# Mixer groups in their own place: a hybrid encoder step with another order of TensorE's small work

## The chip, the cores and the metric

The kernel runs on one core of one Trainium2 chip. The metric is the device time of one execution in microseconds; the median over runs is compared. Matrix products run on TensorE, elementwise work on VectorE (DVE), ScalarE (ACT) and GpSimd (POOL), and most transfers are issued by SyncE (SP).

## The reference

One layer of a streaming encoder is applied to a prompt of 1024 tokens without history and to 32 tokens of a running stream with states. D is 1024. The mixer splits one input projection into three groups of heads, each of which runs a causal recurrence in blocks; the feed-forward part is a gated one with a causal convolution.

```
proj = rms_norm(x) @ w_in                     # split in 15 parts
o_a = gated_linear_scan(q, k, v, log_a, s)    # GLA: 6 heads, dk 32, dv 64
o_b = gated_linear_scan(q, k, v, log_f, s)    # HGRN2: 5 heads, 64 x 64
o_c = mlstm_scan(q, k, v, log_f, ig, c, n, m) # mLSTM: 5 heads, 64 x 64, matrix memory c
cat = concatenate([head_rms_norm(o_a) * silu(gr), head_rms_norm(o_b) * silu(hg),
                   head_rms_norm(o_c) * sigmoid(mo)])
x = x + rms_norm(cat @ w_out)
up = causal_dwconv(rms_norm(x) @ w_up)        # 2 x 2816 wide, 3 taps
x = x + rms_norm((gelu(gate) * val) @ w_down)
...
# inside a scan, per block of L = 64 tokens:
o = scores @ v + (q * exp(b)) @ S             # within the block, and from the state
S = exp(b_last) * S + (k * exp(b_last - b))^T @ v
```

It returns both outputs and all final states.

## The kernel before

**Stages.** The tokens go through the input projection in three groups (`inproj`, g = 0, 1, 2: three, three and two units of 128 prompt tokens, and the 32 sample tokens with the last). Then comes the output projection unit by unit (`outproj`), then the feed-forward part. Every big product is done in three matmuls on split operands (`mm3`: high by high L101, low L102 and L103). The order of units in the output projection is 0, 1, 2, 3, 8, 4, 5 and then 6, 7; unit 8 is the sample.

**Input projection.** Feature-major results are the tiles `pf`; token-major ones are `pv`. In the last group, `vg_across` computes a token-major block in two transposed halves (24 matmuls of 288 columns each, ScalarE copies a half to `vf`), and `back` transposes a whole block to tokens in `pb` (L455), from where `vg_store` passes it on: for the later blocks tanh on ScalarE, a VectorE step on the one tile `vth` (L429), a product on GpSimd (L431), and a store.

**Mixers.** The generator `mixer` runs the recurrence of one unit. `merge` pumps it as side work: units 0 to 2 beside the projection of group 1, units 3 to 5 beside group 2, units 8, 6, 7 beside the output projection. On TensorE a unit is a sequence of small groups: `sc_0`, `sc_2`, `sc_4` (scores at two levels of distance each; `keys`, `memory_scores` and `states` follow them as `mi` and `sm`), then `og` and `oh` (outputs of the two scans, with the memory update `mi` behind them), then `oi` and `om` (memory outputs: from the state `C`, and by the weights `w` within the block). VectorE writes masked scores into `P` (L807), which `og` reads. `finish` turns `og` and `oh` into rows of `cat`: square (ACT L989), sum (DVE L990), root (POOL L220, L221), product (DVE L992), gate (POOL L994). `om` and `oi` of a unit use the two buffers (tag "o") that `og` and `oh` leave after L992. `cat` goes to `cat_d` in memory and comes back as `ct`; `outproj` transposes it (`ctp`, L1076) for its products `zp`. Unit 7's `cat` stays in place. The next unit's `qkb` is loaded into a single buffer, and `qe` (ACT L814) is made from it.

**Order.** A scheduler simulates the program and, on each engine, takes the ready instruction with the lowest priority number; the number is the place in the program. `tc.high_priority(offset=n)` lowers it by n, and `tc.issue_after(x)` keeps an instruction behind x. All mixer matmuls go through `soon` (L717 to 719), which chains those of a group one behind the other.

Of the kernel before, what the change touches and what calls it, by code (L numbers as in the profile page):

```python
# [91 lines left out]
def body(ctx: ExitStack, tc: tile.TileContext, a: dict):  # L92
    nc = tc.nc
    act, dve, pool, pe, sp = nc.scalar, nc.vector, nc.gpsimd, nc.tensor, nc.sync
# [5 lines left out]
    def mm3(ps, lh, rh, first, last, **kw):  # L100
        pe.matmul(ps, lh[0], rh[0], start=first, stop=False, **kw)  # L101
        pe.matmul(ps, lh[0], rh[1], start=False, stop=False, **kw)  # L102
        return pe.matmul(ps, lh[1], rh[0], start=False, stop=last, **kw)  # L103
# [175 lines left out]
    def units_of(g):  # L279
        t0, pl, sl = GROUPS[g]  # L280
        us = [(t0 // 128 + i, 128 * i, 128) for i in range(pl // 128)]
        if sl:
            us.append((8, pl, sl))
        return us
# [72 lines left out]
    def inproj(g, xh, xl, normed, scaled=None):  # L357
# [47 lines left out]
        def vg_weights(blk):  # L405
            parts = [(a["w_tok0"][:, ks[0]:ks[-1] + 1], ks, lt0_d[:, ks[0]:ks[-1] + 1]) for ks in VG0] if not blk else \
                [(a["w_tok"][blk - 1, hf], range(4 * hf, 4 * hf + 4), lt_d[blk - 1, hf]) for hf in range(2)]
            ws = []
            for i, (src, ks, low) in enumerate(parts):
                wh, wl, _ = weights(src, p1, f"wt{g}_{blk}_{i}", [128, len(ks), 256 if blk else 282],  # L410
                                    raw=wraw.pop((blk, i), None), eng=dve if VGD[g](blk, i) else pool, low=low, kept=g > 0)
                ws += [(wh[:, k], wl[:, k]) for k in range(len(ks))]
            return ws

        def vg_store(blk, u, off, n, ps):
            o = mx.tile([128, 256], F32, tag="vg", name=f"vg{u}_{blk}", bufs=3)
            t = t0 + off
            if blk < 4:
                vcopies.append(act.copy(o[:n], ps[:n, :256]))
                act.dma_start(v_d[t:t + n, 256 * blk:256 * blk + 256], o[:n])  # L420
                return
            c0 = 256 * (blk - 4)
            th = mx.tile([128, 256], F32, tag="vth", name=f"vth{u}_{blk}", bufs=1)
            ia = tanh(th[:n], ps[:n, :256], 0.5)
            ns = min(max(704 - c0, 0), 256)
            if ns:
                iv = dve.scalar_tensor_tensor(th[:n, :ns], th[:n, :ns], 1.0, ps[:n, :ns], op0=ALU.add, op1=ALU.mult)
            if ns < 256:
                iv = dve.tensor_scalar(th[:n, ns:], th[:n, ns:], 1.0, None, op0=ALU.add)  # L429
            vgi[:] = ia, iv  # L430
            pool.tensor_tensor(o[:n], th[:n], gh[:n, c0:c0 + 256], op=ALU.mult)  # L431
            pool.dma_start(g_d[t:t + n, c0:c0 + 256], o[:n])
# [13 lines left out]
        def vg_across(blks):  # L446

            def back(blk, fs):
                us = units_of(g)
                whole = psb.tile([128, 2, 256], F32, tag="big", name=f"pb{us[0][0]}_{blk}")  # L450
                rest = psb.tile([128, 256], F32, tag="big", name=f"pb8_{blk}")
                pss = [whole[:, 0], whole[:, 1], rest]
                for (u, off, n), ps in zip(us, pss):
                    for e in range(2):
                        pe.transpose(ps[:n, 128 * e:128 * e + 128], fs[e][:, off:off + n], ident)  # L455
                for (u, off, n), ps in zip(us, pss):
                    vg_store(blk, u, off, n, ps)

            before = None
            for blk in blks:  # L460
                ws = vg_weights(blk)
                fs = p1.tile([128, 2, T], F32, tag="x", name=f"vf{blk}", bufs=3)
                fs = [fs[:, 0], fs[:, 1]]
                for e in range(2):
                    ps = psb.tile([128, T], F32, tag="big", name=f"pv{g}_{blk}_{e}")
                    for k in range(8):
                        mm3(ps, [w[:, 128 * e:128 * e + 128] for w in ws[k]], (xh[:, k, :], xl[:, k, :]), k == 0, k == 7)
                    act.copy(fs[e], ps)
                    if before and e:
                        back(*before)  # L470
                    yield
                before = (blk, fs)
                yield
            back(*before)
# [215 lines left out]
        if sl:  # L690
            yield from vg_across(range(1, 8))
            return
# [17 lines left out]
    AHEAD = 100  # L710
    LNA = 100

    SOON = 400

    line = [None]

    def soon(fn, *args, **kw):  # L717
        with tc.high_priority(offset=SOON), tc.issue_after(line[0].ins) if line[0] else ExitStack():
            line[0] = fn(*args, **kw)  # L719

    def mixer(u, g, ci0):
        n = 128 if u < 8 else DEC
        t0 = 128 * u
        chunks = [(0, 64), (64, 64)] if u < 8 else [(0, DEC)]
        cl = chunks[0][1]
# [16 lines left out]
        vmt = vm[0]  # L742
# [103 lines left out]
        def scores(sc, c, L, Q, at):  # L846
            for j in (3, 0, 1, 2):
                for (o, m) in chunks:
                    for hf in range(2):
                        f, q0, q1, p0 = HALVES[hf][j]  # L850
                        r = slice(64 * hf, 64 * hf + 64)
                        mm = c if c == levels[0] else m
                        soon(pe.matmul, sc[o:o + mm, p0:p0 + q1 - q0, at:at + m // 2], L[r, f, o:o + mm],
                             Q[r, q0:q1, o // 2:(o + m) // 2], start=True, stop=True)
# [6 lines left out]
        def keys():  # L861
            for f0 in (0, 2):
                kps = small(2, 128)
                for f in (f0, f0 + 1):
                    soon(pe.transpose, kps[:n, f - f0, :], khf[:, f * n:f * n + n], ident)
                for ch, (o, m) in enumerate(chunks):
                    with tc.high_priority(offset=AHEAD):
                        act.copy(kt2[o:o + m, ch, 128 * f0:128 * f0 + 256], kps[o:o + m].rearrange("p f n -> p (f n)"))

        w = mx.tile([128, 320], F32, tag="w", name=f"w{u}", bufs=1)  # L870
        w3 = w[:n, :5 * cl].rearrange("p (h n) -> p h n", n=cl)

        def memory_scores():
            sm = psm.tile([128, 6, 64], F32, tag="o", name=f"sm{u}", bufs=2)
            for f in range(3):
                rows, hs = (128, slice(2 * f, 2 * f + 2)) if f < 2 else (64, slice(4, 5))
                for (o, m) in chunks:
                    soon(pe.matmul, sm[o:o + m, hs, :m], mk[:rows, f, o:o + m], mqz[:rows, hs, o:o + m], start=True, stop=True)
            kp = small(4, 64)
            for f in range(2):  # L880
                soon(pe.transpose, kp[:n, 2 * f:2 * f + 2, :].rearrange("p h d -> p (h d)"), mk[:, f, :], ident)
            soon(pe.transpose, sm[:n, 5, :], mk[:64, 2, :], ident[:64, :64])
            for (h0, h1, kp) in ((0, 4, kp), (4, 5, sm[:, 5:6])):
                for ch, (o, m) in enumerate(chunks):
                    kwi[0] = dve.tensor_tensor(kw2[o:o + m, ch, h0:h1], kp[o:o + m, :h1 - h0],
                                               cols[o:o + m, 96 + h0:96 + h1].unsqueeze(2).broadcast_to([m, h1 - h0, 64]), op=ALU.mult)
            dve.tensor_tensor(w3, w3, sm[:n, :5, :cl], op=ALU.mult)
# [79 lines left out]
        for (h0, h1, ot) in ((0, 6, og), (6, 11, oh)):  # L967
            for h in range(h0, h1):
                f, r0, dk, vc = HEADS[h]
                for ch, (o, m) in enumerate(chunks):  # L970
                    soon(pe.matmul, ot[o:o + m, OUT[h], :], P[o:o + m, PLANE[h], :m], v[o:o + m, vc:vc + 64],
                         start=h == h0, stop=False, skip_group_check=True)
        for (h0, h1, ot) in ((0, 6, og), (6, 11, oh)):
            for h in range(h0, h1):
                f, r0, dk, vc = HEADS[h]
                for ch, (o, m) in enumerate(chunks):
                    soon(pe.matmul, ot[o:o + m, OUT[h], :], qz[:, h, o:o + m], Ss[ch][:, f, :],
                         start=False, stop=h == h1 - 1, skip_group_check=True)
# [23 lines left out]
        om = psm.tile([128, 5, 65], F32, tag="o", name=f"om{u}", bufs=2)  # L1002
        oi = psm.tile([128, 5, 65], F32, tag="o", name=f"oi{u}", bufs=2)
        line[0] = None
        for h in range(5):
            for ch, (o, m) in reversed(list(enumerate(chunks))):
                soon(pe.matmul, oi[o:o + m, h, :], mqz[:, h, o:o + m], Cs[ch][:, h // 2, :], start=True, stop=True)
        for h in range(5):
            for ch, (o, m) in enumerate(chunks):
                soon(pe.matmul, om[o:o + m, h, :], w[o:o + m, h * cl:h * cl + m], vmt[o:o + m, h, :], start=True, stop=True)  # L1010
        yield
        hn = mx.tile([128, 5, 65], F32, tag="hn", name=f"hn{u}", bufs=1)
        dve.tensor_tensor(hn[:n], oi[:n], cols[:n, 32:37].unsqueeze(2).broadcast_to([n, 5, 65]), op=ALU.mult)
# [677 lines left out]
    def mixers(g):  # L1691
        us = [(u, 2 * i) for i, (u, off, n) in enumerate(units_of(g))]
        return chain_of(*[mixer(u, g, c) for (u, c) in us[-1:] + us[:-1]]) if us[-1][0] == 8 else \
            chain_of(*[mixer(u, g, c) for (u, c) in us])
# [252 lines left out]
```

## Time and profile before

| | |
|---|---|
| median of 3 runs | 1396.19 us (1401.11, 1394.82, 1396.19) |
| profiled execution | 1395.19 us, span 1393.4 us |
| granted TensorE clock, mean | 0.979 |
| TensorE busy | 1316.8 us, 95% |
| VectorE / ScalarE / GpSimd busy | 1022.0 / 704.4 / 329.2 us |

Busy time of TensorE is matmuls; weight loads overlap them. A wait in brackets behind an instruction names the instruction that ended it and is idle time of the engine ahead of the one listed. The input projection of groups 1 and 2 lies at about 140 to 500 us, its end and the output projection at 500 to 725, the feed-forward part behind that.

### The profile page before, as it was taken

To read this page: it belongs to the slowest core of one execution; us is meant where nothing else is said; L and a number is where in the kernel's file an instruction comes from. 1 tells how busy PE (TensorE), PEld (TensorE's weight loads), DVE (VectorE), ACT (ScalarE), POOL (GpSimd) and SP (SyncE) were. 2 spreads that over 40 slices of the span, in tenths; PEclk is the share of its full clock that TensorE was granted. 3 is DMA by queue.
4 is the path that set the end of the run, shared out by engine and by line. 5 is a ranking of instruction groups with operands and counts; after the bars stand their busy time and mean duration, and the time that the engine had idled before them with its cause. 6 is when DMAs were issued, how large, how long until landed. Compare 5 with 4: busy or idle time off the path is not lost.

```text
span 1393.4 us, 29184 instructions
## 1 busy us (share of the span) xinstructions
PE 1316.8 (95%) x11472; PEld 1197.7 (86%) x11472; DVE 1022.0 (73%) x1916; ACT 704.4 (51%) x1368; POOL 329.2 (24%) x529
## 2 busy tenths in 40 slices
PE   6999999999899897989989999999999999999997
PEld 5999889899788795867779999999999997678885
DVE  4787676956669527787678888888888886399566
ACT  4456455635466335443465555555455454354552
POOL 5532410315303225332121111211121110010005
PEclk9999999999999998999999999999999999999998
DMA  9599777777587964534323555735564329744435
GB/s 344 195 332 365 242 255 248 243 257 249 166 279 257 333 212 158 162 106 162 123 65 123 167 149 134 178 115 144 151 157 120 105 93 376 309 160 129 144 114 121
DMA packets 125825, 269.72 MB, mean 194 GB/s; under 512 B 24007, under 2 KB 59367, under 8 KB 125607
## 3 DMA queue, kind: packets, MB, share of 16 engines
q1 hardware_dynamic: 111959, 245.43, 51.7%
q0 software_dynamic: 8928, 18.09, 7.1%
q10 hardware_dynamic: 4800, 4.33, 0.9%
q8 instruction: 90, 1.47, 0.4%
q14 instruction: 48, 0.39, 0.1%
HBM read 206.72 MB, written 86.18 MB: 210 GB/s over the span
## 4 chain that ended last, share of the span: by engine, by line
PE 72%; DVE 12%; DMA 6%; ACT 5%; issue 2%; POOL 2%; SPq 0%; DVEq 0%; ACTq 0%; POOLq 0%
PE pux L103 4%; PE pux L102 4%; PE pux L101 4%; PE pv L101 3%; PE puw L102 3%; PE puw L101 3%; PE puw L103 3%; PE pv L103 3%; PE pv L102 3%; PE q L101 3%; PE q L102 3%; PE q L103 3%; PE x L101 2%; DMA qkb<-qkb_d 2%; PE x L102 2%
## 5 line engine op out<-in xcount | busy, mean ns | idle before, releaser
L1370 DVE SCALAR_TENSOR_TENSOR y<-uu,fconv_sb,y 128x1060 f32<-128x1060 f32 x88 | 116.3, 1321 | 36.9 <-ACT y L1368 36.0
L1306 ACT COPY c<-pux 128x272 f32<-128x272 f32 (+1 forms) x132 | 49.6, 377 | 48.0 <-PE pux L103 47.3
L101 PE MATMUL pv<-wt_0h,xh 128*128 128x256 f32 (+2 forms) x195 | 58.2, 299 | 7.4 <-ACT xh L321 6.2
L101 PE MATMUL zp<-woh,ch 128*128 128x512 f32 (+1 forms) x144 | 59.0, 413 | 4.1 <-DVE z L1185 2.9
L1368 ACT ACTIVATE y<-uu,fconv_sb 128x1060 f32<-128x1060 f32 x44 | 56.0, 1273 | 7.6 <-POOL uu L1364 7.1
L103 PE MATMUL zp<-woh,cl 128*128 128x512 f32 (+1 forms) x144 | 58.4, 406 | 0.7 <-DVE cl L1081 0.6
L1367 POOL COPY fhalo<-uu 128x2 f32<-128x2 f32 x44 | 16.5, 376 | 178.6 <-DVE uu L1311 178.5
L102 PE MATMUL zp<-wol,ch 128*128 128x512 f32 (+1 forms) x144 | 58.4, 406 | 0.0
L103 PE MATMUL pv<-wt_0h,xl 128*128 128x256 f32 (+2 forms) x195 | 57.1, 293 | 0.6 <-DVE xl L322 0.6
L102 PE MATMUL pv<-wt_0l,xh 128*128 128x256 f32 (+2 forms) x195 | 57.0, 292 | 0.1
L103 PE MATMUL pv<-wt_1h,xl 128*128 128x256 f32 (+2 forms) x195 | 56.9, 292 | 0.0
L102 PE MATMUL pv<-wt_1l,xh 128*128 128x256 f32 (+2 forms) x195 | 56.8, 291 | 0.0
L101 PE MATMUL pv<-wt_1h,xh 128*128 128x256 f32 (+2 forms) x195 | 56.7, 291 | 0.0
L220 POOL TENSOR_SCALAR hrs<-hss 128x5 f32<-128x5 f32 (+3 forms) x27 | 13.0, 483 | 179.4 <-DVE hss L990 178.5
L431 POOL TENSOR_TENSOR vg<-vth,gh 128x256 f32<-128x256 f32 (+1 forms) x36 | 31.3, 870 | 93.4 <-DVE vth L429 26.3
L1546 POOL TENSOR_TENSOR gss<-gss 128x1 f32<-128x1 f32 (+1 forms) x9 | 8.1, 897 | 185.2 <-ACT gjk L1539 185.2
L807 DVE COPY_PREDICATED P<-masks_sb,sc 128x352 f32<-128x352 int32 (+3 forms) x53 | 38.0, 716 | 17.7 <-PE sc L719 16.5
L101 PEld LDWEIGHTS pv<-wt_0h,xh 128*128 128x128 f32 (+1 forms) x195 | 37.5, 192 | 9.9 <-ACT xh L321 7.4
L103 PEld LDWEIGHTS pv<-wt_0h,xl 128*128 128x128 f32 (+1 forms) x195 | 37.7, 193 | 1.4 <-DVE xl L322 1.2
L102 PEld LDWEIGHTS pv<-wt_0l,xh 128*128 128x128 f32 (+1 forms) x195 | 37.6, 193 | 0.8 <-POOL wt_0l L110 0.5
L103 PEld LDWEIGHTS pv<-wt_1h,xl 128*128 128x128 f32 (+1 forms) x195 | 37.6, 193 | 0.8 <-issue 0.4
L221 POOL TENSOR_TENSOR hrs<-hrs,mhalf 128x5 f32<-128x5 f32 (+3 forms) x27 | 37.7, 1395 | 2.3
(1713 smaller groups left out, 5312.5 us busy)
## 6 DMA issues: line engine op xcount, KB each, us to landing
wrP<-in_w_dn SPq DMA_DIRECT2D x27, 512.0 KB, 4.8
h_d<-y SPq DMA_DIRECT2D x22, 530.0 KB, 4.1
ht<-h_d SPq DMA_DIRECT2D x22, 530.0 KB, 10.3
wt_0r<-in_w_tok SPq DMA_DIRECT2D x21, 512.0 KB, 6.3
wt_1r<-in_w_tok SPq DMA_DIRECT2D x21, 512.0 KB, 5.3
ws_d<-in_w_dn POOLq DMA_DIRECT2D x20, 512.0 KB, 9.4
wrP<-ws_d SPq DMA_DIRECT2D x20, 512.0 KB, 4.0
wt_0l<-lt_d SPq DMA_DIRECT2D x14, 512.0 KB, 5.8
```

Of the source, the lines that this page charges most:

```text
L101: pe.matmul(ps, lh[0], rh[0], start=first, stop=False, **kw)
L102: pe.matmul(ps, lh[0], rh[1], start=False, stop=False, **kw)
L103: return pe.matmul(ps, lh[1], rh[0], start=False, stop=last, **kw)
L220: pool.tensor_scalar(out, ss, 1.0 / width, eps, op0=ALU.mult, op1=ALU.add)
L221: pool.tensor_tensor(out, out, mhalf[:n, :cols], op=ALU.pow)
L431: pool.tensor_tensor(o[:n], th[:n], gh[:n, c0:c0 + 256], op=ALU.mult)
L807: dve.copy_predicated(dst, mk.broadcast_to([n, 11, *mk.shape[2:]]), src)
L1306: kept[name] = act.copy(t, ps)
L1367: behind["POOL"] = pool.tensor_copy(fhalo[:, j, :], u[:, NCOL - 2:NCOL])
L1368: act.activation(y, u, AF.Identity, scale=fconv[:, j, 2:3], bias=fconv[:, j, 3:4])
L1370: dve.scalar_tensor_tensor(y, uu[i][:, s:s + NCOL], fconv[:, j, s:s + 1], y, op0=ALU.mult, op1=ALU.add)
L1546: pool.tensor_tensor(ss[:n, 0:1], ss[:n, 2:3], ss[:n, 3:4], op=ALU.add)
```

## The change

Three edits. Mixer matmuls are no longer numbered 400 places ahead, only chained. Of the memory outputs, `om` is issued ahead of `oi`. In `vg_across` the transposes of the block before come after the first half of the next block, not after its second.

```diff
-                    if before and e:
+                    if before and not e:
                         back(*before)
...
-    SOON = 400
-
     line = [None]
 
     def soon(fn, *args, **kw):
-        with tc.high_priority(offset=SOON), tc.issue_after(line[0].ins) if line[0] else ExitStack():
+        with tc.issue_after(line[0].ins) if line[0] else ExitStack():
             line[0] = fn(*args, **kw)
...
         for h in range(5):
+            for ch, (o, m) in enumerate(chunks):
+                soon(pe.matmul, om[o:o + m, h, :], w[o:o + m, h * cl:h * cl + m], vmt[o:o + m, h, :], start=True, stop=True)
+        for h in range(5):
             for ch, (o, m) in reversed(list(enumerate(chunks))):
                 soon(pe.matmul, oi[o:o + m, h, :], mqz[:, h, o:o + m], Cs[ch][:, h // 2, :], start=True, stop=True)
-        for h in range(5):
-            for ch, (o, m) in enumerate(chunks):
-                soon(pe.matmul, om[o:o + m, h, :], w[o:o + m, h * cl:h * cl + m], vmt[o:o + m, h, :], start=True, stop=True)
```

The lines of the changed program are numbered two lower from `soon` on (L717 for L719, L1074 for L1076). Big products are the rows of L101 to L103; their total count and that of the small ones is the same. Three places of TensorE's order follow.

The first is unit 3, on TensorE, where the second projection group turns into the third: `mi` is the memory update of the unit, `pv5_7` the last token-major block of group 1, `pf2` and `pv6` products of group 2. Before:

```order
L719 MATMUL mi_158<-vm0_157,kw2_156 64x65 x10
L103 MATMUL pv5_7_4261<-wt1_7_1h_4159,xl1_1706 128x256
...
L318 MATMUL xt60_4311<-ident_122,x6_3354 128x128 x4
L318 MATMUL xt61_4318<-ident_122,x6_3354 128x128 x4
L101 MATMUL pv6_0_4343<-wt2_0_0h_4327,xh2_4308 128x282
L102 MATMUL pv6_0_4343<-wt2_0_0l_4328,xh2_4308 128x282
L719 MATMUL oi3_5087<-C3_0_4917,mqz_155 64x65
...
L719 MATMUL om3_5086<-vm0_157,w3_4561 64x65 x10
L103 MATMUL pv6_0_4343<-wt2_0_0h_4327,xl2_4309 128x282
```

And now:

```order
L717 MATMUL mi_158<-vm0_157,kw2_156 64x65 x10
L101 MATMUL pf2_3_4931<-xh2_4308,wf2_3h_4927 128x288
...
L103 MATMUL pf2_0_5057<-xh2_4308,wf2_0l_5054 128x288
L717 MATMUL om3_5086<-vm0_157,w3_4561 64x65 x10
L717 MATMUL oi3_5087<-C3_0_4917,mqz_155 64x65
...
L717 MATMUL oi3_5087<-C2_1_4115,mqz_155 64x65
L101 MATMUL pf2_4_5114<-xh2_4308,wf2_4h_5110 128x288
```

12 big products stood between the memory update and the outputs (ten of `pv5_7`, two of `pv6`); now 72 do, and `om` leads.

The second is TensorE's turn from the last projection group to the output projection: `pv2_7` are the halves of block 7, `pb` the blocks transposed back (from `vf6` and `vf7`), `ctp00` and `ctp01` the transposes of unit 0's rows. Before:

```order
L103 MATMUL pv2_7_0_6746<-xh2_4308,wt2_7_1l_6742 128x288
L101 MATMUL pv2_7_1_6772<-xh2_4308,wt2_7_0h_6735 128x288
...
L103 MATMUL pv2_7_1_6772<-xh2_4308,wt2_7_1l_6742 128x288
L455 MATMUL pb6_6_6798<-ident_122,vf6_6654 128x128 x4
L455 MATMUL pb8_6_6799<-ident_122,vf6_6654 32x128 x2
L455 MATMUL pb6_7_6827<-ident_122,vf7_6745 128x128 x4
L455 MATMUL pb8_7_6828<-ident_122,vf7_6745 32x128 x2
L1076 MATMUL ctp00_6867<-ident_122,ct0_5748 128x128 x4
L1076 MATMUL ctp01_6876<-ident_122,ct0_5748 128x128 x4
L101 MATMUL zp00_6907<-woh_6857,ch00_6872 128x512
```

And now, where `sm8` and `mi` are small groups of unit 8:

```order
L455 MATMUL pb6_6_6772<-ident_122,vf6_6654 128x128 x4
...
L455 MATMUL pb8_6_6773<-ident_122,vf6_6654 32x128 x2
...
L101 MATMUL pv2_7_1_6801<-xh2_4308,wt2_7_0h_6735 128x288
...
L717 MATMUL sm8_7091<-ident_122,mqk8_6888 32x64
L455 MATMUL pb6_7_6827<-ident_122,vf7_6745 128x128 x3
L455 MATMUL pb8_7_6828<-ident_122,vf7_6745 32x128 x2
L1074 MATMUL ctp00_6867<-ident_122,ct0_5748 128x128 x4
...
L717 MATMUL mi_158<-v8_6893,kt2_154 64x64 x5
L1074 MATMUL ctp01_6876<-ident_122,ct0_5748 128x128 x4
L101 MATMUL zp00_6907<-woh_6857,ch00_6872 128x512
```

Block 6 is transposed back before the second half of block 7 is multiplied, and groups of unit 8 come in between block 7, `ctp00` and `ctp01`.

The third is unit 7, the last mixer, on TensorE in the output projection: `mi` is its memory update, `zp81` are products of unit 8, `zp50` of unit 5; `fxt` transposes a finished unit for the feed-forward part. Before:

```order
L719 MATMUL mi_158<-vm0_157,kw2_156 64x65 x10
L102 MATMUL zp81_8284<-wol_6858,ch80_7846 32x512
...
L103 MATMUL zp81_8284<-woh_6857,cl81_7982 32x512
L1076 MATMUL ctp41_8333<-ident_122,ct4_7839 128x128 x4
L1180 MATMUL fxt30_8342<-ident_122,z3_7795 128x128 x4
L719 MATMUL oi7_8312<-C7_0_8250,mqz_155 64x65
...
L719 MATMUL om7_8311<-vm0_157,w7_7915 64x65 x10
```

And now:

```order
L717 MATMUL mi_158<-vm0_157,kw2_156 64x65 x10
L1178 MATMUL fxt81_8465<-ident_122,z8_8082 128x32 x4
L717 MATMUL om7_8311<-vm0_157,w7_7915 64x65 x10
L101 MATMUL zp50_8486<-woh_6857,ch50_8419 128x512
...
L102 MATMUL zp50_8486<-wol_6858,ch51_8455 128x512
L717 MATMUL oi7_8312<-C7_0_8250,mqz_155 64x65
```

14 products of unit 8's `zp81` stood between the memory update and the outputs; now `om` follows after four transposes, and `oi` 14 products of `zp50` later.

## The prediction

> **What bounds the kernel now.** I read the engine line of the page first, then the stretches by stage, then TensorE's list of waits, then the single matmuls behind the waits that the change can touch.
>
> ```profile
> PE 1316.8 (95%) x11472; PEld 1197.7 (86%) x11472; DVE 1022.0 (73%) x1916; ACT 704.4 (51%) x1368; POOL 329.2 (24%) x529
> 0.00:140.00 140.00, 125.41 (x896) 119.28 (x897) 99.15 (x150) 75.66 (x134) 58.97 (x63) 1.00 0.88 309
> 140.00:360.00 220.00, 206.59 (x2611) 193.06 (x2612) 157.23 (x366) 113.90 (x234) 66.44 (x90) 0.98 0.75 249
> 360.00:500.00 140.00, 127.79 (x1588) 116.64 (x1587) 93.45 (x262) 75.26 (x177) 29.34 (x43) 0.94 0.78 264
> 500.00:725.00 225.00, 200.59 (x1815) 163.61 (x1814) 155.66 (x298) 107.91 (x235) 73.55 (x103) 0.95 0.43 136
> 725.00:1393.40 668.40, 656.39 (x4574) 605.11 (x4572) 516.52 (x843) 331.64 (x590) 100.90 (x232) 0.99 0.52 156
> ```
>
> The columns of a stretch are its length, busy TensorE, weight loads, VectorE, ScalarE and GpSimd, then the granted clock, the DMA share and GB/s. TensorE bounds the kernel everywhere. The change keeps its instructions, so only its idle time and its clock can move: 76.6 us of idle time in all (1393.4 - 1316.8), of which 13.4 lie in 140 to 360, 12.2 in 360 to 500 and 24.4 in 500 to 725, the three stretches where mixers run. The FFN (from 725) holds no mixer group. So some 50 us is all that there is to fight for, and the list says for 140 to 730 us who is waited for:
>
> ```profile
> PE om L719 <- DVE cat L992: 8.6, 5, 2.6
> PE oi L719 <- DVE cat L992: 7.9, 4, 6.3
> ...
> PE ctp L1076 <- DVE vth L429: 3.8, 1, 3.8
> ...
> PE pb L455 <- DVE vth L429: 2.1, 1, 2.1
> PE og L719 <- DVE P L807: 1.7, 1, 1.7
> PE ctp L1076 <- DVE cl L1081: 1.4, 1, 1.4
> PE sc L719 <- DVE P L807: 1.0, 2, 0.6
> ```
>
> (Total us, times, longest.) 16.5 us is one kind of wait: a unit's memory outputs `oi` and `om` write the two buffers that `og` and `oh` leave, and `finish` must first square, reduce, take the root and multiply into `cat`. 7.3 us (2.1 + 3.8 + 1.4) is one place, the turn from the third projection group to the output projection. The single waits:
>
> ```profile
> 178.48 0.80 PE L719 MATMUL om<-vm,w 64*64 64x65 f32 x20 [1.57 <-DVE cat L992]
> 254.57 0.80 PE L719 MATMUL om<-vm,w 64*64 64x65 f32 x20 [2.55 <-DVE cat L992]
> 359.84 0.80 PE L719 MATMUL oi<-C,mqz 128*64 128x65 f32 x20 [1.23 <-DVE cat L992]
> 362.79 1.35 PE L719 MATMUL om<-vm,w 64*64 64x65 f32 x20 [2.15 <-DVE cat L992]
> 430.03 1.19 PE L719 MATMUL om<-vm,w 64*64 64x65 f32 x20 [1.62 <-DVE cat L992]
> 477.40 1.35 PE L719 MATMUL oi<-C,mqz 128*64 128x65 f32 x20 [6.26 <-DVE cat L992]
> ```
>
> They are units 0, 1, 3, 3, 4 and 5: 15.4 of the 16.5 us. The clock falls around them:
>
> ```profile
> 255.60:262.40 6.80, 6.80 (x32) 6.80 (x30) 6.80 (x19) 5.55 (x13) 1.59 (x3) 0.75 0.68 196
> 361.00:371.20 10.20, 8.41 (x78) 8.10 (x79) 10.13 (x31) 4.86 (x13) 2.23 (x3) 0.67 0.17 48
> 429.00:435.80 6.80, 5.77 (x58) 5.28 (x62) 6.74 (x19) 4.60 (x12) 1.73 (x4) 0.75 0.64 227
> 476.60:483.40 6.80, 5.99 (x60) 5.74 (x61) 4.86 (x18) 2.85 (x10) 3.18 (x4) 0.64 1.04 408
> 527.60:537.80 10.20, 5.97 (x21) 4.54 (x22) 6.92 (x15) 6.23 (x11) 4.18 (x7) 0.67 0.80 249
> ```
>
> Length times (1 - clock) is 1.7 + 3.4 + 1.7 + 2.4 + 3.4 = 12.6 us at most, less where TensorE idled anyway.
>
> **The change, part by part.** By the order of instructions nothing is added or removed. Counted in big products (the matmuls of L101 to L103), the mixer groups of the projection come 140 to 210 products later, in the output projection 46 to 62. What matters is the distance from a unit's `og` group to the first of its memory outputs: unit 0 goes from 26 products to 72, unit 1 from 45 to 62, unit 3 from 12 to 72; unit 2 stays (71, 72), unit 4 falls from 57 to 35 for the first and stands at 61 for the second, unit 5 stays at 24, unit 7 falls from 14 to 0 for `om` and stays at 14 for `oi`. What a product is worth:
>
> ```profile
> 467.02 0.41 PE L101 MATMUL pv<-xh,wt_0h 128*128 128x288 f32 x1
> 470.19 0.30 PE L103 MATMUL pv<-xh,wt_1l 128*128 128x288 f32 x1
> ```
>
> and, in the output projection:
>
> ```profile
> 641.88 0.48 PE L101 MATMUL zp<-woh,ch 128*128 128x512 f32 x1
> 647.21 0.39 PE L103 MATMUL zp<-woh,cl 128*128 128x512 f32 x1
> ```
>
> Both pairs are first and last of 24: 3.3 us in the projection (0.14 each), 5.6 us in the output projection (0.23).
>
> *Units 0, 1, 3.* 46, 17 and 60 more products are 6.4, 2.4 and 8.4 us of cover for waits of 1.57, 2.55 and 3.38 us: 7.4 gained.
>
> *Unit 4.* 22 fewer products let the first output wait up to 3 us, the second, 26 products on, no more: 1.6 become about 2. Counted at nothing.
>
> *Unit 5.* Same 24 products, so the chain of `finish` decides. In it the square stands behind the next unit's `qe` on ScalarE, which waited for a load:
>
> ```profile
> 472.44 0.96 ACT L814 ACTIVATE qe<-qkb,cf_sb 128x32 f32<-128x32 f32 x4 [8.47 <-DMA qkb<-qkbs_d]
> 473.30 0.47 ACT L989 ACTIVATE sq<-og 128x384 f32<-128x384 f32 x1
> ```
>
> `qe` still stands ahead of the square in ScalarE's order. The load starts when the unit's last scores are read; these now stand 24 products ahead of `og` (19 before), so a little earlier. Between 0 (as before) and 6.3 (gone) I take half, 3.1. Outputs together: 10.5 of 16.5, bounds 6 and 16.5. `om` ahead of `oi` by itself is worth nothing I can see: both need a buffer, and whichever comes first gets the one that is free first.
>
> *Clock.* Of the 12.6 us, the stretches at 255 and 361 and half of those at 429 and 476 lie at waits that go: 5.1 + 2.0 = 7.1, less the 1.8 + 0.9 in which TensorE idled in those rows. That is 4.4; I take 4, bounds 0 and 9. The first row has no idle TensorE of its own; the wait of 2.55 us just ahead of it was enough for half the clock in half of 6.8 us. [...]
>
> *The turn to the output projection.* `pb` of the last two blocks stood back to back in front of `ctp`, with one tile `vth` to pass through tanh, VectorE and GpSimd. Now block 6 is transposed after the first half of block 7, 24 products or 3.3 us earlier, and groups of unit 8 stand between the last `pb` and `ctp`. Of 7.3 us and a clock of 0.67 I take 5.5 as gained, bounds 1 and 9.
>
> *Unit 7, the price.* `sc` of its last level, `og` and `om` now follow each other with only state products and a few transposes between:
>
> ```profile
> 627.30 1.77 PE L719 MATMUL mi<-v,kt 128*32 128x64 f32 x44
> 627.40 2.94 DVE L807 COPY_PREDICATED P<-masks_sb,sc 128x352 f32<-128x352 int32 x3 [3.31 <-PE sc L719]
> ```
>
> and, for `om`:
>
> ```profile
> 634.54 0.86 PE L719 MATMUL mi<-vm,kw 128*64 128x65 f32 x20
> 637.00 0.56 DVE L992 TENSOR_TENSOR cat<-og,hrs 128x384 f32<-128x384 f32 x1
> ```
>
> `og` needs P, whose third copy ended at 630.34, 1.3 us after the state products (629.07). `om` needs `cat`, 637.56, 2.2 after the memory products (635.40). Before, 24 output products filled these gaps; now 3.5 us are bare, bounds 0 and 6.
>
> *Unit 8, the price.* Its outputs stood 108 products ahead of the transposes `ctp` of its rows (through `cat_d` and back), now 72. 36 x 0.23 = 8.3 us of cover go. No wait of `ctp` for that load is in the list, so the bounds are 0 and 8.3; I take 4.
>
> *Other gates* (`og` and `sc` on P, 2.7 us now): 2.5 more, bounds -2 and 6.
>
> Sum: 10.5 + 4 + 5.5 = 20 gained, 3.5 + 4 + 2.5 = 10 paid, net -10. The profiled execution took 1395.2 us (span 1393.4, 1.8 around it), 1.0 under the median 1396.2. 1395.2 - 10 + 1.0 = 1386. With each term's bounds taken together only in part: 1374 to 1398.
>
> **The rivals.**
>
> *Waits gone altogether, 1369.* All 16.5 of the outputs, 4 of clock, 9 at the turn, and only the 2.5 paid: -27, 1395.2 - 27 + 1.0 = 1369. For it: later groups have their operands lying ready for longer. Against: unit 5's distance is the same.
>
> [...]
>
> *The waits only move, 1393.* Units 4, 5 and 7 wait more by what 0, 1 and 3 wait less, unit 8's load takes the clock gain; only part of the turn's 5.5 remains: -3. For it: `finish` passes four engines and nothing in it gets faster.
>
> *Slower, 1409: VectorE between score groups.* Where a unit's groups stand 24 products apart, the next scores wait until VectorE has taken the last ones and written the operands again:
>
> ```profile
> L807 DVE COPY_PREDICATED P<-masks_sb,sc 128x352 f32<-128x352 int32 (+3 forms) x53 | 38.0, 716 | 17.7 <-PE sc L719 16.5 <-ACT P L957 0.5
> L841 DVE TENSOR_TENSOR Qz<-x,qe 128x128 f32<-128x128 f32 (+1 forms) x98 | 24.5, 286 | 10.4 <-PE sc L719 9.4 <-ACT x L836 0.9
> L832 DVE TENSOR_TENSOR Ld<-x,qkb 128x256 f32<-128x256 f32 (+1 forms) x40 | 17.2, 429 | 7.1 <-PE sc L719 7.0
> ```
>
> Two copies (1.4) and two levels of operands (2 x (0.43 + 3 x 0.29) = 2.6) make 4.0 us, about 8 on a VectorE that is 70% busy with other work, against some 5 us of products and small groups. 3 us at 11 gates of units 5, 8, 6 and 7 is 33 paid against 20 gained: +13, 1409. It decides from about 20 us of such waits. Against it: units 6 and 7 had gates 10 to 36 products apart before, and the list has only 1.0 + 1.7 us for them. For it: in the projection the distance was mostly above 24, and there the products are shorter.
>
> That the change does not move the groups is excluded by the order.
>
> **How the numbers follow.** Forecast 0.42, waits gone 0.13, no clock gain 0.04, waits only move 0.18, VectorE 0.23. About 0.5%, 7 us, is what a measurement of this kernel can tell from no change: faster is below 1389, slower above 1403. A fifth of the forecast's 0.42 reaches over 1389, so faster is 0.34 + 0.13 = 0.47, same 0.08 + 0.04 + 0.18 = 0.30, slower 0.23. The range goes from the gain case's 1369, less 3 for part of the clock that it leaves, to the slower case's 1409, and leaves out the half of that case that lies above.
>
> **What would show it.** Right: no waits of `om` and `oi` for `cat` in units 0, 1 and 3, a granted clock of 1.00 after them, `pb` and `ctp` waiting under 2 us together, and a new wait of 2 to 4 us at unit 7's `og` and `om`. Wrong: waits of `sc` or `og` for P of over 10 us in total, a wait of unit 8's `ctp` for its load over 8 us, or unit 5's wait still at 6 with the clock of 0.64 behind it.

## The result, and the profile after

The changed kernel takes 1377.49 us (median of 4 runs, 1375.92 to 1379.31), the kernel before 1398.05 us (1394.82 to 1401.11): a ratio of 0.9854, interval 0.9823 to 0.9884. About 20 us are gained. Ratios here and below leave out two executions of later kernels, one of 4734 us (the profiled one of the row casts) and one of 1455 us at a granted clock of 0.84. The profiled executions stand 16.2 us apart (1395.19 and 1379.03): that of after is near its kernel's upper end, that of before near its lower one.

The stretches between two landmarks come first: from 140 us to the first `zp` (the projection with its mixers), and from there to the first `puy` (the output projection). Before:

```profile
140.00:533.70 393.70, 360.73 (x4429) 333.96 (x4428) 260.29 (x649) 200.63 (x435) 108.81 (x152) 0.96 0.74 247
533.70:683.30 149.60, 139.09 (x1373) 108.17 (x1372) 115.09 (x238) 67.51 (x150) 51.32 (x67) 0.96 0.46 146
```

After, and the engine line of its page:

```profile
140.00:513.90 373.90, 354.01 (x4466) 326.65 (x4464) 269.44 (x655) 201.58 (x437) 106.52 (x153) 0.98 0.76 257
513.90:667.20 153.30, 142.91 (x1393) 111.99 (x1394) 117.28 (x240) 65.98 (x149) 48.62 (x66) 0.94 0.46 144
```

```profile
PE 1313.3 (95%) x11472; PEld 1194.7 (87%) x11472; DVE 1031.8 (75%) x1916; ACT 703.9 (51%) x1368; POOL 325.6 (24%) x529
```

TensorE's idle time fell by 12.6 us (76.6 to 64.0) and its busy time by 3.5, which is read here as clock, since the instructions are the same. The projection is 19.8 us shorter: 13.1 of it idle time, 6.7 busy time. The output projection is 3.7 us longer, and that is busy time at a lower clock (0.94 for 0.96): its idle time is 10.5 us before and 10.4 after. The rest is equal (710.1 us both times). TensorE's list of waits for 140 to 730 us, after:

```profile
PE og L717 <- DVE P L805: 5.2, 3, 2.8
PE pb L455 <- ACT vf L468: 3.9, 2, 3.2
PE zp L101 <- ACT ch L1078: 2.8, 1, 2.8
PE om L717 <- DVE cat L990: 2.7, 2, 1.8
...
PE zp L103 <- DVE cl L1079: 1.9, 1, 1.9
...
PE sc L717 <- DVE Qz L839: 1.5, 1, 1.5
...
PE pb L455 <- DVE vth L427: 1.3, 1, 1.3
...
PE zp L101 <- issue: 1.0, 1, 1.0
...
PE sc L717 <- DVE P L805: 0.9, 1, 0.9
...
PE ctp L1074 <- ACT vth L113: 0.8, 1, 0.8
...
PE oi L717 <- DVE cat L990: 0.3, 1, 0.3
```

The outputs' wait for `cat` fell from 16.5 to 3.0 us. Three things are new or longer. `og` waits for P (5.2 us, 1.7 before). The first block that is transposed back waits for ScalarE's copy:

```profile
434.70 0.40 ACT L812 ACTIVATE qe<-qkb,cf_sb 128x128 f32<-128x128 f32 x1 [8.21 <-DMA qkb<-qkb_d]
...
441.21 0.70 ACT L468 COPY vf<-pv 128x288 f32<-128x288 f32 x2
441.66 1.33 PE L455 MATMUL pb<-ident,vf 128*128 128x128 f32 x5 [3.22 <-ACT vf L468]
```

ScalarE had stood 8.21 us at `qe`, with the copies queued behind it. At the end of the output projection the same engine stands at unit 7's `cat`:

```profile
647.30 1.10 ACT L1221 CAST B21h<-xg 128x1088 fp32r<-128x1088 f32 x1 [3.56 <-POOL cat L992]
...
650.36 1.57 ACT L1078 CAST ch<-ctp 128x512 fp32r<-128x512 f32 x3
651.01 0.50 PE L101 MATMUL zp<-woh,ch 128*128 128x512 f32 x1 [2.76 <-ACT ch L1078]
```

The first cast of the feed-forward part, `B21h`, waits for unit 7's `cat` to end, and the casts of the rows that TensorE needs next stand behind it.

### The profile page after: what moved, and what is told of

Read it like the earlier page. It is cut to its first block, busy times and chain, and to the rows that moved or that the text cites. A ratio compares the mean times of both kernels' runs of the same rounds, so it can differ in the third digit from the quotient of the medians.

```text
span 1377.3 us, 29190 instructions
## 1 busy us (share of the span) xinstructions
PE 1313.3 (95%) x11472; PEld 1194.7 (87%) x11472; DVE 1031.8 (75%) x1916; ACT 703.9 (51%) x1368; POOL 325.6 (24%) x529
## 4 chain that ended last, share of the span: by engine, by line
PE 72%; DVE 11%; DMA 7%; ACT 5%; issue 2%; POOL 2%; SPq 1%; ACTq 0%; DVEq 0%; POOLq 0%
PE pux L103 5%; PE pux L101 5%; PE pux L102 5%; PE puw L101 3%; PE puw L102 3%; PE puw L103 3%; PE pv L101 3%; PE pv L103 3%; PE q L101 3%; PE pv L102 3%; PE q L102 3%; PE q L103 3%; PE x L101 2%; PE x L102 2%; PE x L103 2%
## 5 line engine op out<-in xcount | busy, mean ns | idle before, releaser
L101 PE MATMUL zp<-woh,ch 128*128 128x512 f32 (+1 forms) x144 | 60.5, 422 | 4.8 <-ACT ch L1078 2.8
L101 PE MATMUL pv<-wt_0h,xh 128*128 128x256 f32 (+2 forms) x195 | 57.6, 296 | 5.2 <-ACT xh L321 2.8
L103 PE MATMUL zp<-woh,cl 128*128 128x512 f32 (+1 forms) x144 | 59.0, 410 | 1.9 <-DVE cl L1079 1.9
L1365 POOL COPY fhalo<-uu 128x2 f32<-128x2 f32 x44 | 16.5, 376 | 178.9 <-DVE uu L1309 178.7
L103 PE MATMUL pv<-wt_0h,xl 128*128 128x256 f32 (+2 forms) x195 | 56.0, 287 | 0.2 <-DVE xl L322 0.2
L103 PE MATMUL pv<-wt_1h,xl 128*128 128x256 f32 (+2 forms) x195 | 56.1, 288 | 0.0
L101 PE MATMUL pv<-wt_1h,xh 128*128 128x256 f32 (+2 forms) x195 | 55.9, 287 | 0.0
L220 POOL TENSOR_SCALAR hrs<-hss 128x5 f32<-128x5 f32 (+3 forms) x27 | 9.7, 358 | 175.4 <-DVE hss L988 174.7
L101 PEld LDWEIGHTS pv<-wt_0h,xh 128*128 128x128 f32 (+1 forms) x195 | 36.8, 189 | 7.1 <-ACT xh L321 3.5
L827 ACT ACTIVATE x<-x 128x256 f32<-128x256 f32 (+1 forms) x44 | 17.9, 406 | 43.3 <-DVE x L825 36.1
L101 PEld LDWEIGHTS zp<-woh,ch 128*128 128x128 f32 (+1 forms) x144 | 27.4, 190 | 12.5 <-ACT ch L1078 3.0
L992 POOL TENSOR_TENSOR cat<-cat,gt 128x320 f32<-128x320 f32 (+3 forms) x27 | 31.7, 1174 | 26.4 <-DVE cat L990 26.3
```

The lines of the kernel that those rows point to most:

```text
L827: act.activation(xv[:, :, 0, :], xv[:, :, 0, :], AF.Exp, scale=-1.0)
L992: pool.tensor_tensor(cat[:n, c0:c0 + 64 * nh], cat[:n, c0:c0 + 64 * nh], gt[:n, c0:c0 + 64 * nh], op=ALU.mult)
L1365: behind["POOL"] = pool.tensor_copy(fhalo[:, j, :], u[:, NCOL - 2:NCOL])
```

## The experiments

All ratios are to the kernel before, run beside each. Places means the first edit (no lead of 400), om the second, turn the third. Stage lengths and waits come from one profiled execution of each kernel, the ratios from the medians. The lead of 200 and the three kernels with `qe` held back ran on another chip than the other experiments.

**Turn alone.**

```diff
-                    if before and e:
+                    if before and not e:
```

> The kernel before with only the earlier transposes of the projection's blocks (the third edit alone). Theory A, the prediction's: the turn to the output projection was worth 7.3 us of waits and some clock, so this alone gives 4 to 6 us (ratio 0.996 to 0.997). Rival B: what is gained at the turn is given back where the first block's transposes now wait for ScalarE's copy of the block's second half (3.2 us and a clock of 0.62 behind it in the changed kernel): within 2 us of before (0.9985 to 1.0015).

0.9931 (0.9909 to 0.9954), about twice what theory A said; B is out in time. Only part of it lies at the turn: `pb`, `ctp` and the first `zp` still wait 0.4 + 3.6 + 0.3 us there, of 7.3. Unit 5's outputs moved from 24 to 34 products behind `og` and no longer wait, but most of their 6.26 us has only another name. ScalarE stands as long as before at the next unit's `qe`, and now the copies `vg` behind it hold TensorE:

```profile
470.45 0.96 ACT L814 ACTIVATE qe<-qkb,cf_sb 128x32 f32<-128x32 f32 x4 [8.60 <-DMA qkb<-qkbs_d]
...
473.68 0.61 PE L101 MATMUL pv<-xh,wt_0h 128*128 128x288 f32 x1 [4.71 <-ACT vg L419]
...
476.38 1.35 PE L719 MATMUL oi<-C,mqz 128*64 128x65 f32 x20
```

So part of rival B's mechanism, a wait for ScalarE's copy, is there. The projection is 4.9 us shorter than before and the output projection 4.7; where the rest of the gain comes from is not shown.

**Places alone.**

```diff
-        with tc.high_priority(offset=SOON), tc.issue_after(line[0].ins) if line[0] else ExitStack():
+        with tc.issue_after(line[0].ins) if line[0] else ExitStack():
```

> The kernel before with only the 400 places of lead taken away from the mixer's matmuls (the first edit alone; oi still ahead of om, the transposes where they were). Theory A: the distance from a unit's og group to its memory outputs did it, so 13 to 17 of the 20 us come from this edit (0.988 to 0.991), and the waits of oi and om for cat fall from 16.5 us to under 4. Rival B: the three edits are worth something only together, or om ahead of oi matters: under 8 us (above 0.994).

0.9827 (0.9808 to 0.9845): even more than A said, and the waits of `om` and `oi` are 2.2 + 1.6 = 3.8 us. This edit by itself gains as much as the whole change. The projection takes 379.7 us, the output projection 145.5:

```profile
140.00:519.70 379.70, 358.04 (x4488) 330.70 (x4486) 268.18 (x657) 202.41 (x438) 107.65 (x154) 0.97 0.76 255
519.70:665.20 145.50, 140.24 (x1373) 108.75 (x1372) 116.66 (x238) 67.22 (x150) 43.92 (x66) 0.96 0.47 149
```

**om alone.** Only the two loops are exchanged, in the kernel before.

> The kernel before with om ahead of oi alone. Theory A (the prediction: nothing that I can see, both need a buffer and the first gets the one that is free first): 0.998 to 1.002, with the waits of the two for cat still 15 to 18 us. Rival B: the state C, which oi reads, is late where units follow closely, and om first hides it: 2 to 4 us faster (0.997 to 0.9985).

0.997 (0.9956 to 0.9984): small, at the edge of both. The waits for `cat` are 9.2 + 6.7 = 15.9 us, as A said, so a hidden state `C` isn't seen; where the 4 us come from stays open.

**Places and om**, without the turn; **places and turn**, with `oi` first.

> The changed kernel without its third edit: own places and om first, the transposes of the projection's blocks where they were before. Theory A: the first edit carries all (alone 0.983), and the earlier transposes collide with it in the last units, so this stands with the first edit alone: 0.981 to 0.985, the output projection (first zp to first puy) near 145 us as there, not 153. Rival B: om first is what cost the 0.3%: as the changed kernel, 0.985 to 0.987, with 150 us or more.

0.9906 (0.9884 to 0.9928): outside both. The output projection has the 145.9 us that A expected, and yet it is slower than places alone, by 7.4 us in the projection. Unit 4 shows some of it. In places alone and then here:

```profile
437.32 1.28 ACT L812 ACTIVATE qe<-qkb,cf_sb 128x128 f32<-128x128 f32 x4 [6.92 <-DMA qkb<-qkb_d]
```

```profile
441.28 0.40 ACT L812 ACTIVATE qe<-qkb,cf_sb 128x128 f32<-128x128 f32 x1 [10.32 <-DMA qkb<-qkb_d]
...
450.45 1.29 PE L717 MATMUL om<-vm,w 64*64 64x65 f32 x20 [4.70 <-DVE cat L990]
```

Unit 4's groups stand at the same big products to within two, but the load of the next unit's `qkb` ends later, `qe` with it, and then the squares, `cat` and `om`. It is issued 3.0 us later (434.28 us against 431.32), behind other transfers of SyncE; how the order of `om` and `oi` brings that about was not tried.

> The changed kernel without its second edit: own places and earlier transposes, oi ahead of om as before. Theory A: the order of oi and om is worth nothing, the collision is between the first and the third edit: as the changed kernel, 0.984 to 0.987. Rival B: om first is what cost: 0.975 to 0.982 (the first edit's 1.7% and part of the third's 0.7%).

0.9853 (0.9832 to 0.9874), as the changed kernel: A. In the presence of the turn, the order of `oi` and `om` is worth nothing that these runs can tell. Taken together, the three edits do not add: places 0.983, turn 0.993, om 0.997, all three 0.985. `om` first beside places alone costs (0.991 against 0.983, intervals apart). The intervals of places alone and of all three overlap; that the other two edits together cost something beside the first is likely, not shown.

**The turn for the last block only.**

```diff
-                    if before and not e:
+                    if before and e == (blk < 7):
```

> The changed kernel, but only the last block's predecessor is transposed back early; the other blocks as before. Theory A: the wait of 3.2 us for ScalarE's copy (and about 2 to 3 us of clock behind it) goes, and unit 7's groups come 24 to 36 products earlier, so this beats the changed kernel by 4 to 8 us (ratio to before 0.980 to 0.983). Rival B: the turn alone counted and the wait for the copy just moves on to the next block: as the changed kernel (0.985 to 0.987).

0.9868 (0.9849 to 0.9887): B. `pb`'s wait is gone from the list, and another wait for the same copies has come, of the products that need the buffer:

```profile
PE pv L101 <- ACT vf L468: 4.2, 2, 2.6
```

The outputs' wait for `cat` grew as well, to 2.9 + 3.6 = 6.5 us, from 3.0 in the changed kernel.

**Lead for units 8, 6, 7 again.**

```diff
+        with tc.high_priority(offset=400) if unit[0] in (8, 6, 7) else ExitStack(), tc.issue_after(...)
```

> The changed kernel, with the 400 places of lead given back to units 8, 6 and 7 alone, whose groups then come 48 to 80 big products earlier. Theory A: the output projection's loss (it took 3.7 us longer, with 4.7 us of waits for the casts of unit 6's rows, which stand behind ScalarE's cast of the first feed-forward operand, which waits for unit 7's cat) goes: 4 to 7 us faster than the changed kernel (0.980 to 0.983), and no wait of zp for ch over 1 us at the end. Rival B: the lead of units 8, 6, 7 brings back waits of oi and om for cat in units 8, 6 and 7: as the changed kernel or slower (0.985 to 0.990).

0.9945 (0.9925 to 0.9965): worse than B said. The wait of `zp` for `ch` is gone from the end, as A had it, but the output projection takes 159.5 us:

```profile
517.70:677.20 159.50, 142.73 (x1371) 111.29 (x1372) 116.83 (x239) 67.17 (x149) 47.06 (x66) 0.94 0.44 142
```

TensorE idles 16.8 us there, against 10.4 in the changed kernel, in many places (`sc` 3.8, `fxt` 2.9 and 2.1, `om` 2.2). Rival B's cause, the waits of `om` for `cat`, is only the last of these.

**Row casts ahead of `B21h`.** `B21h` is held behind the casts of unit 6's rows and of the first half of unit 7's.

```diff
+                for u in (6, 7):
+                    cast.enter_context(tc.issue_after(kept[u].ins))
+            halves("B21", q["B21"])
```

> The changed kernel, with ScalarE's cast of the first feed-forward operand (B21h) held behind its casts of the rows of unit 6 and of the first half of unit 7. Theory A: those casts stood behind B21h, which waits for unit 7's cat to end, so zp's waits for ch (2.8 us) and cl (1.9 us) at the end of the output projection go, and with them the clock of 0.56 behind: 3 to 7 us faster than the changed kernel (ratio to before 0.980 to 0.983). Rival B: unit 6's and 7's own chain of finish is as late as B21h, the wait stays under another name: 0.984 to 0.988.

0.9877 (0.9856 to 0.9899): B, no gain; where the wait went stays open.

**A lead of 200 in place of 400.**

```diff
-    SOON = 400
+    SOON = 200
```

> The kernel before with a lead of 200 places in place of 400. Groups stand some 100 to 150 big products earlier than with no lead, but the distances from og to the memory outputs are wide (51, 62, 62, 71, 57, 23 products for units 0 to 5, against 26, 45, 71, 12, 57, 24 with 400 and 72, 62, 72, 66, 57, 35 with none). Theory A (the distance decides): as with no lead, 0.981 to 0.986. Rival B (it is how long operands lie ready ahead of a group, over all groups): about half of the first edit's gain, 0.989 to 0.994.

0.9931 (0.9908 to 0.9954): under half the gain of no lead, as B's number has it, and theory A, that the distance from `og` decides, falls. 12.3 us of the outputs' waits stayed, 7.0 of them at units 1, 2 and 4, where the distance was wide. Unit 1 has the same 62 products from `og` to its outputs here as in the changed kernel. Here, and then there:

```profile
257.86 1.28 ACT L814 ACTIVATE qe<-qkb,cf_sb 128x128 f32<-128x128 f32 x4 [4.90 <-DMA qkb<-qkb_d]
...
263.67 0.47 ACT L989 ACTIVATE sq<-og 128x384 f32<-128x384 f32 x1
...
270.51 1.02 PE L719 MATMUL oi<-C,mqz 128*64 128x65 f32 x20 [2.47 <-DVE cat L992]
```

```profile
265.44 1.28 ACT L812 ACTIVATE qe<-qkb,cf_sb 128x128 f32<-128x128 f32 x4 [8.71 <-DMA qkb<-qkb_d]
...
268.20 0.49 ACT L987 ACTIVATE sq<-og 128x384 f32<-128x384 f32 x1 [0.40 <-PE oh L717]
...
276.07 0.80 PE L717 MATMUL om<-vm,w 64*64 64x65 f32 x20
```

The memory products began at 259.19 us with the lead of 200, and the square came 4.5 us later, behind `qe` and the work queued after it. In the changed kernel they began at 267.72, and the square came 0.5 us later: `qe` was done. That load can start when the last scores are read (unit 5's was issued 0.7 us behind them in the changed kernel); from these to `og` there are 22 products here, 47 in the changed kernel. So two distances seem to count, last scores to `og` (which covers the load) and `og` to outputs (which covers `finish`). It is read from one unit, where 2.1 of the 4.5 us are a wait of ScalarE for VectorE, and no run varied one distance alone; rival B's mechanism was not separated from it.

**`qe` behind the squares**, in three kernels: before, places alone, and all three edits.

```diff
-        with tc.issue_after(vcopies[8].ins) if u == 0 else ExitStack():
+        with tc.issue_after(vcopies[8].ins) if u == 0 else tc.issue_after(outs[0].ins):
```

> The kernel before with ScalarE's qe of a unit held behind the squares of og and oh of the unit before (it stands ahead of them in the kernel before, and waits 8.5 us for a load in unit 8's case). Theory A: unit 5's wait of 6.26 us and the clock of 0.64 behind it came from that place in ScalarE's queue: 5 to 9 us faster (0.9935 to 0.9965), and the longest wait of oi for cat falls under 3 us. Rival B: the chain of finish is as long without it: 0.998 to 1.002.

0.9942 (0.9924 to 0.996): A in time. The longest wait of `oi` is 3.3 us, not under 3, and the waits for `cat` are 12.5 in place of 16.5. The edit is worth some 8 us, but by theory A's mechanism only in part: unit 5's outputs still wait 3.3 + 0.8 of their 6.26 us, and a clock of 0.50 for 6.8 us still lies there (from 465.8 us). Where the rest of the gain lies is not shown.

> The first edit alone (0.983), and qe behind the squares of the unit before. Theory A: what is left of the waits of og's and oh's followers (om and oi for cat 3.8 us) goes, and the copies behind qe on ScalarE come earlier: 2 to 6 us faster than the first edit alone (0.978 to 0.981). Rival B: with own places the distance hides the chain already, and qe, now later, makes the next unit's scores late: 0.982 to 0.987.

0.992 (0.9901 to 0.9939): slower than places alone by more than B said. The waits for `cat` fall to 0.2 us, and the projection takes 379.2 us, about as without the edit (379.7); but the output projection takes 156.5 us at a clock of 0.92:

```profile
519.20:675.70 156.50, 142.95 (x1373) 110.23 (x1372) 117.42 (x239) 66.60 (x150) 43.41 (x67) 0.92 0.48 144
```

Its list of waits for 140 to 720 us:

```profile
PE zp L103 <- DVE cl L1079: 6.3, 2, 4.9
PE pv L101 <- ACT vf L468: 6.2, 1, 6.2
...
PE ctp L1074 <- ACT z L1102: 4.0, 2, 3.7
```

The wait of 6.2 us lies in the projection. There ScalarE stands at another load, that of a weight cast, with the copies `vf` behind it:

```profile
452.28 1.04 ACT L337 CAST wt_1h<-wt_1r 128x1024 fp32r<-128x1024 f32 x1 [6.46 <-DMA wt_1r<-in_w_tok]
453.23 0.39 ACT L468 COPY vf<-pv 128x288 f32<-128x288 f32 x1
```

> The changed kernel, and qe behind the squares of the unit before. Theory A: its wait of 3.2 us for ScalarE's copy of the first block's half (the copy stands behind a qe that waited 8.2 us for its load) and the clock of 0.62 behind it go, and unit 7's groups come some 30 products earlier: 5 to 9 us faster than the changed kernel (0.979 to 0.982). Rival B: the copy stands behind qe still, and nothing but small shifts: 0.984 to 0.988.

0.9894 (0.9865 to 0.9922): not faster than the changed kernel. The copy's wait falls from 3.9 to 2.0 us, but the output projection takes 154.8 us at 0.92. No version tried is shown to beat places alone.

## Why the prediction was right, and where not

The direction, the main term's mechanism and the range held; the forecast of 1386 was 8.5 us too high, a gain of 10 where about 20 came. The measured time lies midway between the forecast and the rival *waits gone altogether* (1369). By its own steps, in the profiled executions:

- *Outputs' waits*: 10.5 of 16.5 forecast, 15.3 gone (the 3.0 that are left hold 1.8 at unit 7, which is priced below). Units 0 and 3 lost theirs, unit 1 all but 0.3, unit 4 half of 1.86, and unit 5 all of its 6.26. For units 0, 1 and 3 the step looked at the distance behind `og` alone; the lead of 200 speaks for a second one, ahead of `og`, which covers the load of `qkb`. For unit 5 the prediction had that load in view and took half; it was the whole, and its reading that the load starts with the last scores was off (below). That `om` first by itself is worth nothing is open: 0.997 alone, 0.991 against 0.983 beside the first edit.
- *Clock*: 4 forecast, and 3.5 measured as busy time over all, but the nearness is luck. In the projection, where the term lay, busy time fell by 6.7; in the output projection, where no cost of clock was forecast, it rose by 3.8. That a wait of 2.55 us is enough for half the clock was the author's reading of one row; no run varied a wait alone, and behind another of 2.55 us the clock was 1.00 (last section).
- *The turn*: 5.5 forecast, about nothing measured. `pb` and `ctp` waited 7.3 us there; now `ctp` waits 0.8 and `zp` 1.0, but the blocks ahead of it wait 3.9 + 1.3. The sign that was set, `pb` and `ctp` under 2 us together, was missed with 6.0. This step failed: it did not ask what the earlier transposes of all the other blocks would wait for. With the turn alone `pb` waits 0.4 us, so it takes the first edit too. The clock there did not gain either (below).
- *Unit 7*: 3.5 forecast, 0.9 (`og`) + 1.8 (`om`) = 2.7 measured.
- *Unit 8*: 4 forecast, none: no `ctp` waits for its load.
- *Other gates*: 2.5 forecast. `og`, `sc` on P and on Qz went from 2.7 to 5.2 + 0.9 + 1.5 = 7.6, less unit 7's 0.9: 4.0. Not foreseen were the 2.8 + 1.9 = 4.7 us of `zp` at the end, behind `B21h`.

For unit 5's load, the last scores ended at 459.1 us before and 473.2 after. Before, SyncE issued the load 6.9 us behind them, after other transfers; now it is 0.7 us, and the square comes 0.4 us ahead of the memory products (481.07), not 7.1 us behind them (466.22). What let SyncE issue it earlier was not tried. Before, and then now:

```profile
466.02 0.38 SPq L731 DMA_DIRECT2D qkb<-qkbs_d  x1
```

```profile
473.88 1.13 SPq L729 DMA_DIRECT2D qkb<-qkbs_d  x1
480.70 0.49 ACT L987 ACTIVATE sq<-og 128x384 f32<-128x384 f32 x1 [0.24 <-PE og L717]
```

At the turn, half the clock lasted 6.8 us before (529.2 to 536.1) and 10.2 now:

```profile
512.00:522.30 10.30, 9.26 (x34) 6.46 (x34) 10.20 (x18) 6.52 (x8) 1.31 (x2) 0.50 0.97 336
```

8.4 us of it now lie behind the first `zp`, 2.4 before. There its products start 0.43 us apart at a clock of 0.50, and 0.23 at 1.00. Counted as half of the 6.0 us between them, that is an estimate of 3.0 of the 3.7 us that the output projection lost. In places and turn it lasted 3.4 us, so how much of it is the change's is open.

The price as a whole was mis-sized. 10 were forecast, 7.5 of them (units 7 and 8) for the output projection, which lost 3.7, and that in clock. Its waits came to as much before as after, 10.5 and 10.4 us, so unit 7's 2.7 and the 4.7 of `zp` were made up by others that went, such as those of `zp` and `fxt` for `z`, which the prediction had not counted as movable (before):

```profile
PE zp L101 <- DVE z L1185: 2.9, 2, 2.6
...
PE fxt L1180 <- DVE z L1185: 2.0, 1, 2.0
```

Most of the longer gates (`og` 2.8 and 1.5, `sc` 0.9) lie in the projection. The prediction's count of how far its groups move, 140 to 210 products, is short as well: by the traces it goes up to some 240. No term rests on it.

Between the profiled executions 16.2 us were gained where 10 were forecast. The other 2.5 us of the miss are the place of the profiled executions: that of before was put 1.0 below its median, that of after stands 1.5 above.

Of the rivals, VectorE between score groups is refuted as a cause of a loss: these gates cost 7.6 us in all, and the point from which they decide was 20. That the waits only move is refuted for the projection, and true in sum for the output projection. That no clock is gained (0.04 in the prediction) is refuted for the projection, by 6.7 us less of busy time and a clock of 0.98 for 0.96.

## What to carry to other kernels

Lead for side work on a priority scheduler is not free (here 1.7%): a group that is issued as early as its operands allow can have its followers close behind, and then each waits for a chain over four engines (16.5 us of such waits before, 3.8 with places alone). What seems to count is cover on each leg of the chain, here the load ahead of the group and `finish` behind it. Look for an engine that stands at a load with others' work queued behind. ScalarE did so ahead of one of the longest new waits of TensorE in the turn alone (4.7 us), the changed kernel (3.2), places and om (4.7) and places with `qe` held back (6.2). With places alone, taking one such place away did not help: another stood behind it. And ask of a wait that is gone whether it has only changed its name. Three edits that are each worth something can be worth less together than the best of them.

## What the runs showed of the hardware

In the kernel before, the clock record has ten dips, each to 0.50. They last 3.4 us or a multiple of it (6.8), but for the last, which runs over the kernel's end. In the 3.4 us ahead of a dip TensorE idled 1.1 to 3.4 us, and only once, at unit 5's wait, all of it. The dip in the prediction's first clock row began at 256.2 us, 1.6 us after the wait of 2.55 us had ended, and lasted 3.4 us. Behind another wait of 2.55 us, which ended at 595.41, the clock was 1.00 for the next 6.8 us. In the dip at 256.2 us the `pf` products of 384 columns started 0.32 us apart, and behind it 0.175. What length or place of a wait brings a dip is not shown.

Once the clock fell where TensorE had not waited at all. In the changed kernel, 1.7 us a row:

```profile
191.50:193.20 1.70, 1.70 (x68) 1.19 (x66) 0.74 (x2) 1.22 (x3) 0.00 (x0) 1.00 0.41 116
193.20:194.90 1.70, 1.70 (x30) 1.58 (x30) 0.97 (x4) 1.52 (x3) 0.00 (x0) 0.91 1.02 383
194.90:196.60 1.70, 1.70 (x26) 1.30 (x24) 1.64 (x2) 1.69 (x2) 0.00 (x0) 0.50 1.03 359
196.60:198.30 1.70, 1.70 (x6) 1.70 (x7) 0.98 (x1) 1.70 (x1) 0.00 (x0) 0.58 0.73 292
198.30:200.00 1.70, 1.70 (x12) 1.70 (x11) 1.56 (x3) 0.60 (x3) 0.00 (x0) 1.00 0.03 12
```

From 191.5 us some 90 small matmuls of unit 0 (64 x 64 scores, 32-row states) ran back to back, TensorE busy in every row, and from 194.6 the clock was 0.50 for 3.4 us. That the small groups cost the clock here is not shown: those of unit 1 in the same trace kept the full clock,

```profile
255.30:258.70 3.40, 3.40 (x110) 2.96 (x108) 1.08 (x2) 1.32 (x2) 0.00 (x0) 1.00 0.93 274
258.70:262.10 3.40, 3.40 (x36) 3.33 (x35) 2.92 (x5) 0.00 (x0) 0.00 (x0) 1.00 0.97 369
```

and so did those of unit 0 with places alone (1.00 in each row from 193.2 to 200.0 us). No experiment varied the groups.
